# Ring slots of 16 KB a partition, and the experts' weights in rows of 16 KB

## The chip, the cores and the metric

The kernel runs on one core of one Trainium2 chip. A core has five engines that run their own instruction streams: PE (TensorE, matrix products), DVE (VectorE), ACT (ScalarE), POOL (GpSimd) and SP (SyncE, which here does nothing but issue transfers), and 16 DMA engines that move data between HBM and the on-chip memory SBUF, which has 128 partitions. The metric is the device time of one execution in microseconds, the median of three runs. The profiler takes one execution more, and its trace is what is read below.

## The reference

Two transformer blocks on 256 tokens of width 1024, in fp32. The first has a token mixer (differential attention beside a gated linear recurrence, with a context of 256 tokens) and then a mixture of experts in which each expert chooses its tokens:

```
aff = softmax(h @ w_router)                       # 256 tokens x 16 experts
top_aff, top_idx = top_k(aff.T, 32)               # each expert takes 32 tokens
xin = h[top_idx]                                  # 16 x 32 x 1024
y = (silu(xin @ w_gate) * (xin @ w_up)) @ w_down  # each w: 1024 x 1024 per expert
out = scatter_add(y * top_aff)                    # back to the tokens
```

Each expert has three matrices of 4 MB (MB is 2^20 bytes where nothing else is said), so the 16 have 192 MB. The second block has two layers, an attention with a low-rank projection and one with a window, each with a cross attention to a memory of 256 rows and an MLP of width 4096 with squared relu; a last norm follows.

## The kernel before

The work stands in three stages: the mixer of the first block (`first_mixer`, about 0 to 345 us), routing and experts (`route` and `experts`, to about 820 us), and the second block.

All large weights come through one object, the `Ring` (L76). `queue_loads` (L1634) lists every load in the order in which it will be used. `open` fills the slots of a pool as the pool is made; after that `done(key)`, called behind the last matmul that reads a piece, frees its slot and puts the next load of the list into it (`load`, DMA at L99, issued by SP). That load waits on SP for the semaphore of that last matmul. A slot has 2048 floats in each of the 128 partitions, 1 MB. The numbers of slots stand in one line at the file's end: RA 3 slots for the whole run, RE 7 in the mixer only, 4 (`ringB`) from the end of the mixer on, RX 6 from then until after expert 1, RC 5 and RD 3 from the end of the mixer until after expert 13. So when the experts start, the ring has 21 slots, later 15, and in the second block 7.

An expert (loop at L1007 in `experts`) has 32 tokens, so PE's array is used in four column groups of 32: the groups j work on four quarters of the 1024 hidden columns at once. The loop over q takes a quarter of the 1024 rows of gate, then the same quarter of up, 1 MB each; after each comes a `ring.done`. Such a quarter is 8 products, which the trace shows as 16 PE instructions, as each fp32 product is two. The product's moving operand is a piece of a row of weights (`w`), the stationary operand the tokens (`xin`). Then silu and product on ACT and DVE (`ge`, L1031 to L1035), a transpose through PE (`hT`, copied to `hs`), and the down product in four pieces of 1 MB (`pd`, L1049), each with its `done`. `sT`, copied to `S`, is the matrix that scatters the 32 rows back; `eacc` (L1058) adds the expert's rows `yp` into four accumulators that live through all experts.

For expert 0 each quarter gathers its tokens first (`gather`, tile `gp`, L932); the tokens of experts 4 to 9 are gathered behind expert 1 and those of 10 to 15 behind expert 2. From expert 4 on, pieces of the memory's projections (`memory_kv`) stand behind experts as side work. Behind the last expert comes a norm (`rms_add`), and the second block begins with the transposes `ntp` (L1146).

Of the kernel before, what the change touches and what calls it, by code (L numbers as in the profile page):

```python
# [9 lines left out]
F32 = mybir.dt.float32  # L10
# [9 lines left out]
P = 128  # L20
# [55 lines left out]
class Ring:  # L76


    def __init__(self, nc):
        self.nc = nc  # L80
        self.queue = []
        self.held = {}
        self.closed = set()
        self.n = 0

    def want(self, key, src, part=0, parts=1):

        self.queue.append((key, src, part, parts))

    def load(self, pool):  # L90

        self.n += 1
        t = pool.tile([P, 2048], F32, tag="ring", name=f"ring{self.n}")
        while True:
            key, src, part, parts = self.queue.pop(0)
            _, kk, n = src.shape
            if not part:
                self.held[key] = t[:, : parts * kk * n].rearrange("p (k n) -> p k n", k=parts * kk), pool
            self.nc.sync.dma_start(self.held[key][0][:, part * kk:part * kk + kk], src)  # L99
            if not self.queue or not self.queue[0][2]:  # L100
                break

    def open(self, pool, n):
# [8 lines left out]
        return self.held[key][0]  # L112

    def done(self, *key, later=False):
        _, pool = self.held.pop(key)
        if self.queue and id(pool) not in self.closed:
            if later:
                self.later = pool
            else:
                self.load(pool)  # L120


class K:
# [132 lines left out]
def first_mixer(k, perm, st, ringA):  # L256

    nc, tc, A, ring = k.nc, k.tc, k.A, k.ring
# [30 lines left out]
    ident, vecT, x = st["ident"], st["vecT"], st["x"]  # L289
# [11 lines left out]
    for name, r0, nr in (("b_ada", 0, 8), ("norm_pre_mix", 8, 4)):  # L301
        src = A[name]
# [422 lines left out]
        nc.scalar.copy(vd[tk], pts[tk])  # L725

    es_h.close()
    ringB = st["es_b"].enter_context(tc.tile_pool(name="ringB", bufs=4, side="right", reuse_waits="tile"))
    st["ringX"] = st["es_x"].enter_context(tc.tile_pool(name="ringX", bufs=RX, side="right", reuse_waits="tile"))
    ring.open(st["ringX"], RX)  # L730
    ring.open(ringB, 4)


    def first_gate(i):
# [258 lines left out]
def experts(k, st, moe, pool, ps, routed, side):  # L993

    nc, A, ring = k.nc, k.A, k.ring
    ident, x = k.ident, st["x"]
    iot, aff, slot, xin, gather = routed

    def wk(name, shape=(P, 512)):
        return ps.tile(list(shape), F32, tag="mm", bufs=4, name=k.nm(name))  # L1000

    def small(name, shape, dt=F32, bufs=2):
        return pool.tile(list(shape), dt, tag=name, bufs=bufs, name=k.nm(name))


    acc = [[ps.tile([P, 512], F32, tag="acc", bufs=4, name=k.nm("eacc")) for _ in range(2)] for _ in range(2)]
    for e in range(16):  # L1007
        es_ = slice(32 * e, 32 * e + 32)
        pg, pu = wk("pg", (P, 256)), wk("pu", (P, 256))
        for q in range(4):  # L1010
            if e == 0:
                for hk in (2 * q, 2 * q + 1):
                    gather(hk, 0, 4)
            for nm, pt in (("gate", pg), ("up", pu)):
                w = ring.get(nm, e, q // 2, q % 2)
                for kk in range(2):
                    hk = 2 * q + kk
                    for j in range(4):
                        nc.tensor.matmul(pt[32 * j:32 * j + 32, :], lhsT=xin[:, hk, es_], rhs=w[:, kk, 256 * j:256 * j + 256],  # L1019
                                         start=hk == 0, stop=hk == 7)  # L1020
                ring.done(nm, e, q // 2, q % 2)

        sT = wk("sT", (P, 256))
        for T in range(2):
            rep = small("rep", (P, P))
            nc.vector.tensor_scalar(rep.rearrange("p (a b) -> p a b", a=4), iot[:, None, :].to_broadcast([P, 4, 32]), slot[:, T, e:e + 1], aff[:, T, e:e + 1], op0=ALU.is_equal, op1=ALU.mult)
            nc.tensor.transpose(sT[:, T * P:T * P + P], rep, ident)
        S = small("S", (P, 256))
        nc.scalar.copy(S, sT)
        ge = small("ge", (P, 256))  # L1030
        nc.scalar.activation(ge, pg, AF.Exp, scale=-1.0)  # L1031
        nc.scalar.activation(ge, ge, AF.Ln, bias=1.0)
        nc.scalar.activation(ge, ge, AF.Exp, scale=-1.0)  # L1033
        nc.vector.tensor_tensor(ge, ge, pg, op=ALU.mult)  # L1034
        nc.vector.tensor_tensor(ge, ge, pu, op=ALU.mult)  # L1035

        ht = wk("hT", (P, 256))
        for c in range(2):
            nc.tensor.transpose(ht[:, c * P:c * P + P], ge.rearrange("p (n c) -> p c n", c=2)[:, c, :], ident)
        hs = small("hs", (P, 256))  # L1040
        nc.scalar.copy(hs, ht)

        pd = wk("pd")
        for g in range(4):
            wd = ring.get("down", e, g)
            for c in range(2):
                for n in range(2):
                    j = 2 * n + c
                    nc.tensor.matmul(pd[32 * j:32 * j + 32, :], lhsT=hs[:, c * P + 32 * g:c * P + 32 * g + 32],  # L1049
                                     rhs=wd[:, c, n * 512:n * 512 + 512], start=g == 0, stop=g == 3)  # L1050
            ring.done("down", e, g)
        yp = small("yp", (P, 512))
# [581 lines left out]
def queue_loads(k):  # L1634
# [37 lines left out]
    for e in range(16):  # L1672
        gv = A["w_gate"][0, e].rearrange("(h p k) n -> p h k n", h=2, k=4)
        uv = A["w_up"][0, e].rearrange("(h p k) n -> p h k n", h=2, k=4)
        for h in range(2):
            for i in range(2):
                ring.want(("gate", e, h, i), gv[:, h, 2 * i:2 * i + 2])
                ring.want(("up", e, h, i), uv[:, h, 2 * i:2 * i + 2])
        dv = A["w_down"][0, e].rearrange("(g p k) n -> p g k n", g=4, k=2)
        for g in range(4):  # L1680
            ring.want(("down", e, g), dv[:, g])
        if e in (SM + 1, SM + 3):
            cols(("memkv", (e - SM) // 2), A["w_mem_kv_2"][(e - SM) // 2], 0)
    mi = A["mla_w_in_2"][0].rearrange("(h p k) n -> p h k n", h=2, k=4)
# [2 lines left out]
    for i in range(3):  # L1687
        ring.want(("uq", i), A["mla_w_uq_2"][0].rearrange("(k p) n -> p k n", p=P)[:, i:i + 1])
    for i in range(2):
        ring.want(("ukv", i), A["mla_w_ukv_2"][0].rearrange("(k p) n -> p k n", p=P)[:, i:i + 1])  # L1690
    for l in range(2):
        if l:
            for b in (2, 1, 0):
# [116 lines left out]
```

## Time and profile before

| | us |
|---|---|
| median of three runs | 1404.04 (1404.03 to 1404.29) |
| the profiled execution | 1401.51 |
| its span (first to last instruction) | 1399.7 |
| PE busy | 1234.6 (88%) |
| PE weight loads (PEld, beside PE) | 901.0 (64%) |
| DVE busy | 686.8 (49%) |
| ACT busy | 559.8 (40%) |

SP's loads (DMA queue q1) are 346.86 MB (of 10^6 bytes) and took 66.0% of the 16 DMA engines' span. Busy shares are means over three stages with different limits, so they don't tell what a change in one stage is worth; the rows below cut the span into pieces. A matmul row has the tile it writes, an arrow and what it reads; "128x256 f32 x16" is the shape read and the count of instructions.

### The profile page before, as it was taken

The page shows a single profiled execution, that of the slowest core. Times are in us where ns is not written, and L with a number is a line of the kernel's source. Part 1 is how long each engine was busy: PE and PEld are TensorE (multiplying, and loading weights), DVE is VectorE, ACT ScalarE, POOL GpSimd, SP SyncE. Part 2 cuts the span into 40 slices and gives each one's busy share as a digit, 9 for nine tenths or more (in the row PEclk, how much of TensorE's full clock was granted, in tenths as well). Part 3 has the DMA queues.
Part 4 walks back from the last instruction along what each step waited for, and adds up shares of the span by engine and source line. Part 5 has one row for each costly group of instructions (what it writes and reads, how often), then busy time and mean ns, then how long its engine had stood idle before and what let it go on. Part 6 is the DMA issues. An engine that isn't in the chain of part 4 may idle for free.

```text
span 1399.7 us, 21652 instructions
## 1 busy us (share of the span) xinstructions
PE 1234.6 (88%) x8547; PEld 901.0 (64%) x8547; DVE 686.8 (49%) x1549; ACT 559.8 (40%) x1279; POOL 63.3 (5%) x101
## 2 busy tenths in 40 slices
PE   5999997998698668787766779999999999999997
PEld 4876676865454224343222258899899888989995
DVE  5566686667412111110100058666565766665655
ACT  3466233465112112121100147556455645555554
POOL 1111000000000000000000011100000003000000
PEclk9999999999899888898888689999999999999999
DMA  9723864654799999999999963435655542356540
GB/s 311 273 90 124 271 207 128 236 210 176 323 419 420 419 420 420 419 420 420 420 420 420 419 268 105 168 121 181 195 180 197 162 148 91 121 184 204 179 140 31
DMA packets 91969, 352.07 MB, mean 252 GB/s; under 512 B 7041, under 2 KB 15906, under 8 KB 66780
## 3 DMA queue, kind: packets, MB, share of 16 engines
q1 hardware_dynamic: 89760, 346.86, 66.0%
q0 software_dynamic: 1344, 3.21, 0.9%
q8 instruction: 67, 1.10, 0.3%
q10 hardware_dynamic: 764, 0.63, 0.1%
q14 instruction: 34, 0.28, 0.1%
HBM read 349.62 MB, written 1.05 MB: 251 GB/s over the span
## 4 chain that ended last, share of the span: by engine, by line
PE 63%; DMA 27%; DVE 6%; ACT 3%; issue 1%; POOL 0%; ACTq 0%; SPq 0%; DVEq 0%; POOLq 0%
DMA ring<-in_w_up_dram 14%; PE macc L173 13%; PE mpu L173 12%; DMA ring<-in_w_down_dram 10%; PE pj L173 9%; PE oacc L173 3%; PE sp L597 2%; PE spu L173 2%; PE gp L932 2%; PE ob L1190 2%; DMA ring<-in_w_gate_dram 1%; PE pg L1019 1%; PE pa L184 1%; PE acc L173 1%; PE pe L567 1%; PE pu L1019 1%
## 5 line engine op out<-in xcount | busy, mean ns | idle before, releaser
L166 DVE TENSOR_TENSOR wlo<-ring,whi 128x512 fp32r<-128x512 f32 (+3 forms) x459 | 302.4, 665 | 236.6 <-ACT whi L165 235.8
L165 ACT CAST whi<-ring 128x512 fp32r<-128x512 f32 (+3 forms) x465 | 272.7, 594 | 280.2 <-PE macc L173 78.0
L173 PE MATMUL mpu<-h,whi 128*128 128x256 f32 x1024 | 183.6, 280 | 0.0
L173 PE MATMUL macc<-whi,a 128*128 128x512 f32 x512 | 163.1, 395 | 0.0
L173 PEld LDWEIGHTS mpu<-h,whi 128*128 128x128 f32 x1024 | 157.3, 188 | 0.9 <-ACT whi L165 0.3
L173 PE MATMUL mpu<-h,wlo 128*128 128x256 f32 x512 | 142.5, 280 | 0.6 <-DVE wlo L166 0.6
L173 PE MATMUL pj<-whi,hT 128*128 128x512 f32 x416 | 135.7, 400 | 0.5 <-ACT kc L678 0.5
L173 PEld LDWEIGHTS macc<-whi,a 128*128 128x128 f32 x512 | 96.0, 188 | 22.8
L1019 PE MATMUL pu<-ring,xin 128*32 128x256 f32 x1024 | 81.1, 435 | 26.7 <-DMA ring<-in_w_up_dram 26.7
L1019 PE MATMUL pg<-ring,xin 128*32 128x256 f32 x1024 | 81.7, 435 | 24.2 <-DMA ring<-in_w_gate_dram 24.2
L173 PE MATMUL macc<-wlo,a 128*128 128x512 f32 x256 | 101.1, 395 | 0.0
L173 PEld LDWEIGHTS mpu<-h,wlo 128*128 128x128 f32 x512 | 96.1, 188 | 1.6 <-DVE wlo L166 1.0
L1049 PE MATMUL pd<-ring,hs 128*32 128x512 f32 x512 | 77.2, 704 | 18.0 <-DMA ring<-in_w_down_dram 10.5
L173 PEld LDWEIGHTS pj<-whi,hT 128*128 128x128 f32 x416 | 78.3, 190 | 18.3 <-ACT whi L165 1.1
L173 PE MATMUL pj<-wlo,hT 128*128 128x512 f32 x208 | 83.0, 399 | 0.0
L1019 PEld LDWEIGHTS pg<-ring,xin 128*32 128x32 f32 x1024 | 31.1, 120 | 71.2 <-DMA ring<-in_w_gate_dram 38.0
L1019 PEld LDWEIGHTS pu<-ring,xin 128*32 128x32 f32 x1024 | 33.5, 121 | 66.0 <-DMA ring<-in_w_up_dram 44.2
L1034 DVE TENSOR_TENSOR ge<-ge,pg 128x256 f32<-128x256 f32 x16 | 6.7, 420 | 139.0 <-ACT ge L1033 139.0
L1058 PE MATMUL eacc<-yp,S 64*128 64x512 f32 x128 | 48.5, 753 | 20.2 <-DVE yp L1054 20.2
L1031 ACT ACTIVATE ge<-pg 128x256 f32<-128x256 f32 x16 | 6.2, 384 | 130.1 <-PE pg L1019 130.1
L173 PEld LDWEIGHTS macc<-wlo,a 128*128 128x128 f32 x256 | 48.0, 188 | 11.0
L1058 PEld LDWEIGHTS eacc<-yp,S 64*128 64x128 f32 x128 | 21.7, 222 | 45.0 <-DVE yp L1054 34.1
(491 smaller groups left out, 1932.2 us busy)
## 6 DMA issues: line engine op xcount, KB each, us to landing
ring<-in_w_gate_dram SPq DMA_DIRECT2D x64, 1024.0 KB, 9.9
ring<-in_w_up_dram SPq DMA_DIRECT2D x64, 1024.0 KB, 19.9
ring<-in_w_down_dram SPq DMA_DIRECT2D x64, 1024.0 KB, 19.9
ring<-in_mlp_w_up_dram SPq DMA_DIRECT2D x32, 1024.0 KB, 6.0
ring<-in_mlp_w_down_dram SPq DMA_DIRECT2D x32, 1024.0 KB, 5.0
ring<-in_w_ada_dram SPq DMA_DIRECT2D x24, 1024.0 KB, 5.8
ring<-in_w_in_dram SPq DMA_DIRECT2D x32, 512.0 KB, 4.2
ring<-in_w_o_dram SPq DMA_DIRECT2D x8, 1024.0 KB, 5.0
```

What stands on the lines that cost most here:

```text
L165: nc.scalar.copy(view(hi[:, :n]), raw)
L166: (eng or nc.vector).tensor_tensor(view(lo[:, :n]), raw, view(fl(hi[:, :n])), op=ALU.subtract)
L173: self.nc.tensor.matmul(out, lhsT=av if a_st else wv, rhs=wv if a_st else av, start=first and i == 0, stop=last and i == 2)
L184: nc.tensor.matmul(pa[32 * g:32 * g + 32, :], lhsT=k.cs[:, 4 * h + g, :], rhs=w[:, g, :], start=h == 0, stop=h == 1)
L567: nc.tensor.matmul(pe.rearrange("p a b -> p (a b)"), lhsT=part[:, hs], rhs=hgm[:, d, 4 * half:4 * half + 4].rearrange("p a b -> p (a b)"), ...
L597: nc.tensor.matmul(sp[:, T, i - a, :], lhsT=kl, rhs=ql, start=True, stop=True)
L932: nc.tensor.matmul(gp, lhsT=x[:, T, :].rearrange("p (h n k) -> p h k n", h=2, k=4)[:, h, kk, :], rhs=oh[:, T].rearrange("p e s -> p (e s)" ...
L1019: nc.tensor.matmul(pt[32 * j:32 * j + 32, :], lhsT=xin[:, hk, es_], rhs=w[:, kk, 256 * j:256 * j + 256], start=hk == 0, stop=hk == 7)
L1034: nc.vector.tensor_tensor(ge, ge, pg, op=ALU.mult)
L1049: nc.tensor.matmul(pd[32 * j:32 * j + 32, :], lhsT=hs[:, c * P + 32 * g:c * P + 32 * g + 32], rhs=wd[:, c, n * 512:n * 512 + 512], start=g ...
L1058: nc.tensor.matmul(acc[T][n], lhsT=S[ns, T * P:T * P + P], rhs=yp[ns, :], start=e == 0, stop=e == 15)
L1190: nc.tensor.matmul(self.ob[:, T, n, :], lhsT=pt[:, b * P:b * P + P], rhs=val(c), start=i == 0, stop=i == len(blocks[T]) - 1)
```

## The change

A slot is now 4096 floats a partition, 2 MB, in two halves. Each half holds what a slot held; the slot is free when both halves are done. The pools are resized: RA 2, RE 3, RB 2 (the 4 of `ringB`), RC 3, RD 1, RX 3: 22 MB at the start of the experts, 16 MB later, 8 MB in the second block.

The experts' loads are listed in pairs: two neighbouring 1 MB pieces of one matrix are moved by one DMA with rows of 16 KB (`pair`), where before each was a DMA with rows of 8 KB. The order of the list changes with it: gate's first half, up's first half, gate's second, up's second, down's two halves (before, gate and up alternated by 1 MB). The other weights are loaded as before, two loads to a slot.

For w_down a row of 16 KB holds four neighbouring rows of the matrix, so a partition must hold four neighbouring hidden columns. Therefore the column groups j no longer take quarters of the hidden columns but every fourth one: the moving operand of gate and up is now read with a step of 4 floats. The transposes `hT` read a contiguous half where they read every second column. S, ge, hs and yp have one buffer each instead of two.

The core of the diff:

```diff
@@ class Ring
     def load(self, pool):
         self.n += 1
-        t = pool.tile([P, 2048], F32, tag="ring", name=f"ring{self.n}")
-        while True:
-            key, src, part, parts = self.queue.pop(0)
+        t = pool.tile([P, 4096], F32, tag="ring", name=f"ring{self.n}")
+        slot = self.n, pool
+        self.left[slot] = 0
+        halves = [t[:, 0:2048], t[:, 2048:4096]]
+        done = None
+        while self.queue and (halves or self.queue[0][2]):
+            key, src, part, parts, pair, last = self.queue.pop(0)
             _, kk, n = src.shape
             if not part:
-                self.held[key] = t[:, : parts * kk * n].rearrange("p (k n) -> p k n", k=parts * kk), pool
-            self.nc.sync.dma_start(self.held[key][0][:, part * kk:part * kk + kk], src)
-            if not self.queue or not self.queue[0][2]:
+                self.held[key] = halves.pop(0)[:, : parts * kk * n].rearrange("p (k n) -> p k n", k=parts * kk), slot
+                self.left[slot] += 1
+            if pair is not None and len(halves) == 1:
+                self.nc.sync.dma_start(t.rearrange("p (k n) -> p k n", k=2 * kk), pair)
+                done = self.queue[0][0]
+            elif key != done:
+                self.nc.sync.dma_start(self.held[key][0][:, part * kk:part * kk + kk], src)
+            if last:
                 break
...
     def done(self, *key, later=False):
-        _, pool = self.held.pop(key)
-        if self.queue and id(pool) not in self.closed:
+        _, slot = self.held.pop(key)
+        self.left[slot] -= 1
+        if not self.left[slot] and self.queue and id(slot[1]) not in self.closed:
@@ experts
-                        nc.tensor.matmul(pt[32 * j:32 * j + 32, :], lhsT=xin[:, hk, es_], rhs=w[:, kk, 256 * j:256 * j + 256],
+                        nc.tensor.matmul(pt[32 * j:32 * j + 32, :], lhsT=xin[:, hk, es_], rhs=w[:, kk, :].rearrange("p (n j) -> p j n", j=4)[:, j, :],
...
-        for c in range(2):
-            nc.tensor.transpose(ht[:, c * P:c * P + P], ge.rearrange("p (n c) -> p c n", c=2)[:, c, :], ident)
+        for g in range(2):
+            nc.tensor.transpose(ht[:, g * P:g * P + P], ge[:, g * P:g * P + P], ident)
...
-        for g in range(4):
-            wd = ring.get("down", e, g)
-            for c in range(2):
-                for n in range(2):
-                    j = 2 * n + c
-                    nc.tensor.matmul(pd[32 * j:32 * j + 32, :], lhsT=hs[:, c * P + 32 * g:c * P + 32 * g + 32],
-                                     rhs=wd[:, c, n * 512:n * 512 + 512], start=g == 0, stop=g == 3)
-            ring.done("down", e, g)
+        for g in range(2):
+            for i in range(2):
+                wd = ring.get("down", e, g, i)
+                for c in range(2):
+                    o = g * P + 32 * (2 * i + c)
+                    for n in range(2):
+                        j = 2 * n + c
+                        nc.tensor.matmul(pd[32 * j:32 * j + 32, :], lhsT=hs[:, o:o + 32],
+                                         rhs=wd[:, c, n * 512:n * 512 + 512], start=g + i == 0, stop=g + i == 2)
+                ring.done("down", e, g, i)
@@ queue_loads
-            for i in range(2):
-                ring.want(("gate", e, h, i), gv[:, h, 2 * i:2 * i + 2])
-                ring.want(("up", e, h, i), uv[:, h, 2 * i:2 * i + 2])
-        dv = A["w_down"][0, e].rearrange("(g p k) n -> p g k n", g=4, k=2)
-        for g in range(4):
-            ring.want(("down", e, g), dv[:, g])
+        dv = A["w_down"][0, e].rearrange("(h p k) n -> p h k n", h=2, k=4)
+        for name, vs in (("gate", (gv, 0)), ("up", (uv, 0)), ("gate", (gv, 1)), ("up", (uv, 1)), ("down", (dv, 0)), ("down", (dv, 1))):
+            v, h = vs
+            for i in range(2):
+                ring.want((name, e, h, i), v[:, h, 2 * i:2 * i + 2], pair=None if i else v[:, h])
@@
-RA, RE, RC, RD, RX, WB = 3, 7, 5, 3, 6, 4
+RA, RE, RB, RC, RD, RX, WB = 2, 3, 2, 3, 1, 3, 4
```

On SP, before, these are the last loads that go into newly opened slots and the first ones that wait for a slot to come free behind PE (a `ring_` tile is one slot's use, after the arrow the matrix, in brackets the semaphores waited for):

```order
L99 DMA ring_3253<-in_w_up_dram 128x2048 [waits DMAHW0_49]
L99 DMA ring_3255<-in_w_down_dram 128x2048 [waits DMAHW1_49,PE_49]
L99 DMA ring_3387<-in_w_down_dram 128x2048 [waits DMAHW2_49,PE_49]
L99 DMA ring_3397<-in_w_down_dram 128x2048 [waits DMAHW3_49,PE_49]
L99 DMA ring_3415<-in_w_down_dram 128x2048 [waits DMAHW4_49,PE_49]
L99 DMA ring_3425<-in_w_gate_dram 128x2048 [waits DMAHW5_49,PE_49]
```

After, the same place on SP:

```order
L108 DMA ring_3209<-in_w_gate_dram 128x4096 [waits DVE_49,PE_49]
L108 DMA ring_3211<-in_w_up_dram 128x4096 [waits DVE_49,Activation_49]
L108 DMA ring_3213<-in_w_down_dram 128x4096
L108 DMA ring_3369<-in_w_down_dram 128x4096 [waits DMAHW0_49,PE_49]
L108 DMA ring_3379<-in_w_gate_dram 128x4096 [waits DMAHW1_49,PE_49]
```

The first reload before is ring_3387, of 1 MB, behind expert 0's first gate quarter; after it is ring_3369, of 2 MB, behind the second gate quarter, which is the second half of its slot.

On PE, at the end of the last expert, before (`x8` counts products that stand one behind the other, each two instructions in the trace):

```order
L1019 MATMUL pg_5937<-ring_5804,xin_3361 32x256 x8
L1019 MATMUL pu_5938<-ring_5823,xin_3361 32x256 x8
L1019 MATMUL pg_5937<-ring_5833,xin_3361 32x256 x8
L1019 MATMUL pu_5938<-ring_5843,xin_3361 32x256 x8
L1019 MATMUL pg_5937<-ring_5853,xin_3361 32x256 x8
L1019 MATMUL pu_5938<-ring_5863,xin_3361 32x256 x8
L1039 MATMUL hT_6028<-ident,ge_6022 128x128 x2
L1049 MATMUL pd_6033<-ring_5873,hs_6031 32x512 x4
L1049 MATMUL pd_6033<-ring_5883,hs_6031 32x512 x4
L1049 MATMUL pd_6033<-ring_5971,hs_6031 32x512 x4
L1049 MATMUL pd_6033<-ring_5981,hs_6031 32x512 x4
```

And after, the same place on PE:

```order
L1032 MATMUL pg_5723<-ring_5588,xin_3319 32x256 x16
L1032 MATMUL pu_5724<-ring_5598,xin_3319 32x256 x16
L1040 MATMUL sT_5797<-ident,rep_5798 128x128
L1040 MATMUL sT_5797<-ident,rep_5801 128x128
L1032 MATMUL pg_5723<-ring_5633,xin_3319 32x256 x16
L1032 MATMUL pu_5724<-ring_5667,xin_3319 32x256 x16
L1052 MATMUL hT_5812<-ident,ge_5806 128x128 x2
L1064 MATMUL pd_5817<-ring_5714,hs_5815 32x512 x8
L1064 MATMUL pd_5817<-ring_5749,hs_5815 32x512 x8
```

From expert 3 on, gate and up now stand in two groups each instead of four, and down in two instead of four, so eight products instead of four stand behind the last slot. In experts 0 to 2 gate and up still change by quarters.

## Rows read from the trace of the kernel before

**Rows 1.** The page, 40 slices of the span: GB/s moved by DMA.
```profile
GB/s 311 273 90 124 271 207 128 236 210 176 323 419 420 419 420 420 419 420 420 420 420 420 419 268 105 168 121 181 195 180 197 162 148 91 121 184 204 179 140 31
```
**Rows 2.** The page, the chain that ended last, by engine and by line.
```profile
PE 63%; DMA 27%; DVE 6%; ACT 3%; issue 1%; POOL 0%; ACTq 0%; SPq 0%; DVEq 0%; POOLq 0%
DMA ring<-in_w_up_dram 14%; PE macc L173 13%; PE mpu L173 12%; DMA ring<-in_w_down_dram 10%; PE pj L173 9%; PE oacc L173 3%; PE sp L597 2%; PE spu L173 2%; PE gp L932 2%; PE ob L1190 2%; DMA ring<-in_w_gate_dram 1%; PE pg L1019 1%; PE pa L184 1%; PE acc L173 1%; PE pe L567 1%; PE pu L1019 1%
```
**Rows 3.** Windows: us, PE, PEld, DVE, ACT, POOL busy (instructions), clock, DMA share, GB/s.
```profile
400.00:500.00 100.00, 79.28 (x774) 44.07 (x766) 18.54 (x51) 21.28 (x54) 1.12 (x2) 0.92 1.01 419
...
700.00:800.00 100.00, 68.16 (x598) 23.31 (x590) 6.38 (x15) 8.00 (x19) 0.00 (x0) 0.78 1.01 420
```
**Rows 4.** The same view, the second block.
```profile
850.00:1400.00 550.00, 537.96 (x3472) 477.86 (x3470) 358.49 (x737) 300.85 (x683) 28.34 (x48) 1.00 0.46 150
```
**Rows 5.** The same view, where the experts begin.
```profile
362.00:364.00 2.00, 0.90 (x5) 0.82 (x5) 1.73 (x8) 0.00 (x0) 0.00 (x0) 0.50 0.00 0
364.00:366.00 2.00, 2.00 (x15) 1.42 (x14) 1.79 (x8) 0.46 (x1) 0.00 (x0) 0.50 0.00 0
366.00:368.00 2.00, 2.00 (x28) 1.02 (x24) 0.48 (x3) 0.00 (x1) 0.00 (x0) 0.59 0.03 8
...
370.00:372.00 2.00, 2.00 (x31) 1.07 (x34) 0.01 (x1) 0.46 (x1) 0.00 (x0) 1.00 1.02 430
```
**Rows 6.** Timeline of SP from 360 us: start, us, line, load, count.
```profile
367.43 4.64 SPq L99 DMA_DIRECT2D ring<-in_w_down_dram  x3
```
**Rows 7.** Timeline of PE, expert 0: start, us, line, tile, shapes, count.
```profile
365.44 1.94 PE L1019 MATMUL pg<-ring,xin 128*32 128x256 f32 x16
...
370.43 1.26 PE L1019 MATMUL pg<-ring,xin 128*32 128x256 f32 x16
371.50 1.05 PE L1019 MATMUL pu<-ring,xin 128*32 128x256 f32 x16
```
**Rows 8.** Windows as in rows 3, early in the mixer.
```profile
30.00:35.00 5.00, 5.00 (x51) 3.78 (x50) 3.35 (x12) 1.94 (x4) 0.00 (x0) 1.00 1.08 358
```
**Rows 9.** Timeline of PE, the last expert's down product and behind it.
```profile
807.80 1.83 PE L1049 MATMUL pd<-ring,hs 128*32 128x512 f32 x8 [0.50 <-DMA ring<-in_w_down_dram]
...
812.78 1.06 PE L1049 MATMUL pd<-ring,hs 128*32 128x512 f32 x8 [0.92 <-DMA ring<-in_w_down_dram]
814.65 4.04 PE L1058 MATMUL eacc<-yp,S 64*128 64x512 f32 x8 [0.81 <-DVE yp L1054]
```
**Rows 10.** Timeline of PE, expert 2 with the gather behind it.
```profile
413.11 1.07 PE L1019 MATMUL pg<-ring,xin 128*32 128x256 f32 x16
...
418.31 1.05 PE L1019 MATMUL pg<-ring,xin 128*32 128x256 f32 x16
...
430.00 6.39 PE L932 MATMUL gp<-oh,x 128*128 128x192 f32 x26
436.32 1.07 PE L1019 MATMUL pg<-ring,xin 128*32 128x256 f32 x16
```
**Rows 11.** Timeline of PE, a product with a two-step moving operand.
```profile
27.94 1.12 PE L211 MATMUL pa<-ring,cs 128*32 128x128 f32 x32
```
**Rows 12.** Groups of weight loads: line, tile, shape, count | busy us, mean ns | idle before.
```profile
L173 PEld LDWEIGHTS mpu<-h,whi 128*128 128x128 f32 x1024 | 157.3, 188 | 0.9 <-ACT whi L165 0.3
...
L932 PEld LDWEIGHTS gp<-oh,x 128*128 128x128 f32 x96 | 23.0, 328 | 5.6 <-issue 5.6
...
L1146 PEld LDWEIGHTS ntp<-ident,x 128*128 128x128 f32 x64 | 9.5, 213 | 6.4 <-DVE x L253 6.0
...
L1039 PEld LDWEIGHTS hT<-ident,ge 128*128 128x128 f32 x32 | 5.0, 207 | 22.9 <-DVE ge L1035 17.7 <-issue 3.6 <-ACT S L1029 1.6
...
L1027 PEld LDWEIGHTS sT<-ident,rep 128*128 128x128 f32 x32 | 3.2, 140 | 6.6 <-issue 6.6
```

More of the change, by code (lines that the diff above doesn't have):

```diff
@@ L83, in __init__, with want @@
         self.closed = set()
+        self.left = {}
         self.n = 0
-    def want(self, key, src, part=0, parts=1):
-        self.queue.append((key, src, part, parts))
+    def want(self, key, src, part=0, parts=1, pair=None, last=False):
+        self.queue.append((key, src, part, parts, pair, last))
     def load(self, pool):
         self.n += 1
-        t = pool.tile([P, 2048], F32, tag="ring", name=f"ring{self.n}")
-        while True:
-            key, src, part, parts = self.queue.pop(0)
+        t = pool.tile([P, 4096], F32, tag="ring", name=f"ring{self.n}")
[5 more added lines that the diff above has]
+            key, src, part, parts, pair, last = self.queue.pop(0)
             _, kk, n = src.shape
             if not part:
-                self.held[key] = t[:, : parts * kk * n].rearrange("p (k n) -> p k n", k=parts * kk), pool
-            self.nc.sync.dma_start(self.held[key][0][:, part * kk:part * kk + kk], src)
-            if not self.queue or not self.queue[0][2]:
+                self.held[key] = halves.pop(0)[:, : parts * kk * n].rearrange("p (k n) -> p k n", k=parts * kk), slot
[6 more added lines that the diff above has]
+            if last:
                 break
@@ L114, in done @@
     def done(self, *key, later=False):
-        _, pool = self.held.pop(key)
-        if self.queue and id(pool) not in self.closed:
+        _, slot = self.held.pop(key)
+        self.left[slot] -= 1
+        if not self.left[slot] and self.queue and id(slot[1]) not in self.closed:
             if later:
-                self.later = pool
+                self.later = slot[1]
             else:
-                self.load(pool)
+                self.load(slot[1])
 class K:
@@ L727, in first_mixer @@
     es_h.close()
-    ringB = st["es_b"].enter_context(tc.tile_pool(name="ringB", bufs=4, side="right", reuse_waits="tile"))
+    ringB = st["es_b"].enter_context(tc.tile_pool(name="ringB", bufs=RB, side="right", reuse_waits="tile"))
     st["ringX"] = st["es_x"].enter_context(tc.tile_pool(name="ringX", bufs=RX, side="right", reuse_waits="tile"))
     ring.open(st["ringX"], RX)
-    ring.open(ringB, 4)
+    ring.open(ringB, RB)
     def first_gate(i):
@@ L1027, in experts @@
             nc.tensor.transpose(sT[:, T * P:T * P + P], rep, ident)
-        S = small("S", (P, 256))
+        S = small("S", (P, 256), bufs=1)
         nc.scalar.copy(S, sT)
-        ge = small("ge", (P, 256))
+        ge = small("ge", (P, 256), bufs=1)
         nc.scalar.activation(ge, pg, AF.Exp, scale=-1.0)
@@ L1037, in experts @@
         ht = wk("hT", (P, 256))
-        for c in range(2):
-            nc.tensor.transpose(ht[:, c * P:c * P + P], ge.rearrange("p (n c) -> p c n", c=2)[:, c, :], ident)
-        hs = small("hs", (P, 256))
+        for g in range(2):
+            nc.tensor.transpose(ht[:, g * P:g * P + P], ge[:, g * P:g * P + P], ident)
+        hs = small("hs", (P, 256), bufs=1)
         nc.scalar.copy(hs, ht)
         pd = wk("pd")
-        for g in range(4):
-            wd = ring.get("down", e, g)
-            for c in range(2):
-                for n in range(2):
-                    j = 2 * n + c
-                    nc.tensor.matmul(pd[32 * j:32 * j + 32, :], lhsT=hs[:, c * P + 32 * g:c * P + 32 * g + 32],
-                                     rhs=wd[:, c, n * 512:n * 512 + 512], start=g == 0, stop=g == 3)
-            ring.done("down", e, g)
-        yp = small("yp", (P, 512))
+        for g in range(2):
[8 more added lines that the diff above has]
+                ring.done("down", e, g, i)
+        yp = small("yp", (P, 512), bufs=1)
         for n, copy in enumerate((nc.vector.tensor_copy, nc.scalar.copy)):
@@ L1674, in queue_loads @@
         uv = A["w_up"][0, e].rearrange("(h p k) n -> p h k n", h=2, k=4)
-        for h in range(2):
+        dv = A["w_down"][0, e].rearrange("(h p k) n -> p h k n", h=2, k=4)
+        for name, vs in (("gate", (gv, 0)), ("up", (uv, 0)), ("gate", (gv, 1)), ("up", (uv, 1)), ("down", (dv, 0)), ("down", (dv, 1))):
+            v, h = vs
             for i in range(2):
-                ring.want(("gate", e, h, i), gv[:, h, 2 * i:2 * i + 2])
-                ring.want(("up", e, h, i), uv[:, h, 2 * i:2 * i + 2])
-        dv = A["w_down"][0, e].rearrange("(g p k) n -> p g k n", g=4, k=2)
-        for g in range(4):
-            ring.want(("down", e, g), dv[:, g])
+                ring.want((name, e, h, i), v[:, h, 2 * i:2 * i + 2], pair=None if i else v[:, h])
         if e in (SM + 1, SM + 3):
@@ L1689, in queue_loads @@
     for i in range(2):
-        ring.want(("ukv", i), A["mla_w_ukv_2"][0].rearrange("(k p) n -> p k n", p=P)[:, i:i + 1])
+        ring.want(("ukv", i), A["mla_w_ukv_2"][0].rearrange("(k p) n -> p k n", p=P)[:, i:i + 1], last=i == 1)
     for l in range(2):
```

## The prediction

> **What bounds the kernel now.** I read first the page's slices and its chain of waits. In the slices the reader is to see three stretches: about 345 us in which the transfers come and go, a plateau of 419 to 420 GB/s, and a last part in which they are mostly idle [rows 1]. The chain gives 27% of the span to DMA, nearly all of it the experts' up and down weights, and 63% to PE, whose lines are those of the mixer and of the second block [rows 2]. The windows settle which of the two holds each stage: from 400 to 500 us the DMA engines are full (share 1.01, 419 GB/s) while PE is busy 79 of 100 us, from 700 to 800 us 68 of 100 [rows 3]; from 850 to 1400 us it is the other way round, PE 538 of 550 us with the DMA share at 0.46 [rows 4]. So a change of the ring is worth something in the middle stage alone: by its rate, by the hole in the stream where the stage begins, and by what follows its last transfer. "MB" below is 2^20 bytes, 2.50 us at 420 GB/s.
>
> The hole is seen in narrow windows: nothing moves from 362 to 366 us, 8 GB/s until 368, the full rate by 370 to 372 [rows 5]. The ring is full, and SP's first load after it is issued at 367.43 [rows 6], when PE is through with the gate quarter that it began at 365.44 [rows 7].
>
> **The rate of the stream.** Of the experts' 192 MB, 170 follow the hole, 170 x 2.50 = 425 us. Rows of 8 KB become rows of 16 KB; no row shows one. The nearest are the short ones: from 30 to 35 us the engines are full (1.08) at 358 GB/s [rows 8] with w_ada's rows of 1 KB and w_in's of 2 KB, two MB of the former to each half MB of the latter, 1138 B on the mean. At 16 engines that is 51 ns a row, and 312 ns for 8 KB at 420 GB/s. The straight line through the two is 9.1 ns and 0.0370 ns a byte, so 16 KB would take 615 ns instead of 624: 1.45%, or 6.1 us of the 425. The other end is nothing, if the engines' limit is in the bytes by then, or if a row of 16 KB is moved in pieces. I take -5 us, near the line's end, since the step from 1 to 8 KB did pay by that line. [...]
>
> **The head.** The ring now opens 11 slots of 2 MB, 22 MB in place of 21, so the stream runs 2.5 us longer before it is full. The first slot comes free not with the first gate quarter but with the second, which shares the slot: today that group begins at 370.43 and the next, up, at 371.50 [rows 7]; with about 0.2 us to the issue, 371.7 in place of 367.43, +4.3 us. Two MB are asked for then and two more a microsecond later, so the stream is full at once, as it is now. Head: +4.3 - 2.5 = +1.8 us. If the slots before it are opened later than now, the 2.5 us are lost; if the later half of the gate isn't what is waited for, the 4.3 are not paid: between 0 and +4.3.
>
> **The tail.** The last load is 2 MB, and 16 PE instructions stand behind its landing instead of 8. Eight took 1.06 us at 812.78 and 1.83 us at 807.80, the clock between the two levels (0.78 of the 2.4 GHz from 700 to 800 us) [rows 3, 9]. So it costs +0.9 (by the spacing of the groups below, 0.86) to +1.8 us; I take +1.3. What comes behind (yp, the four eacc products, the norm) is the same chain. The waits inside an expert don't count: an expert's groups are as many as before, and PE has 20 to 30 us of idle time in 100.
>
> **The strided operand.** Gate and up now read every fourth float of a row of weights as the moving operand, 8 groups of 16 PE instructions in each expert. Contiguous, a group of 16 (256 columns) takes 0.86 us to the next: from 413.11 to 418.31 six steps [rows 10]. Step 2 is in the trace: L211 runs 32 instructions of 128 columns, as much work, in 1.12 us against 1.05 for the contiguous group [rows 10, 11], so step 2 is free. Step 4 shows only in weight loads: gp's, which read x with it, take 328 ns against 188 for mpu's contiguous ones, 1.74 times; of the transposes ntp with step 4 takes 213 against 140 for the contiguous sT, and hT with step 2 takes 207 [rows 12]. Weight loads therefore pay for any step, and for 4 nearly what they pay for 2; as moving operands pay nothing for 2, I take nothing for 4. The other end is 1.74 times, worked out in the first rival, and up to 2.3 times, if a moving read with step costs what the two-step transpose shows per column ((207-140) ns over 128 on top of the 0.42 ns of a column). Nothing hides the groups in experts 0 to 2, where PE sets the pace; behind them PE's idle time does. [...]
>
> **The rest.** hT's weight loads become contiguous (207 to 140 ns, two an expert, where PE waits for a transfer anyway). S, ge, hs and yp fall from two buffers to one; each is written after the previous expert's products on PE, which is in order, and beside a DMA wait: nothing. SP issues half as many loads for the experts. In the mixer the ring holds ten MB as before, freed two at a time; of the chain's 27% DMA the lines of rows 2 leave 2% for all else, so nothing; if two MB were wanted before they are there, it is up to 5 us. In the second block the ring has 8 MB in place of 7 and PE shows no wait for it [rows 4]: nothing; if slots of 2 MB came free too late there, a load of 2 MB is 5 us, but the DMA share of 0.46 leaves twice that.
>
> Sum: -5 + 1.8 + 1.3 = -1.9 us. The profiled execution took 1401.51 us (span 1399.7 and 1.8 around it), so 1399.6 by its clock; the median of the runs is 2.5 us above it, 1404.04, and the same -1.9 gives 1402.1. Of this case alone, with rate 0 to -6.1, head 0 to 4.3 and tail 0.9 to 1.8: about 1399 to 1405, the corners left out.
>
> **Rivals.** *The strided operand is slow, s times* (slower than before). Gate and up of an expert take 8 x 0.86 = 6.9 us, so each grows by 6.9(s-1). Experts 0 to 2 are paced by PE; expert 3 starts at 436.32 [rows 10] and would start 20.7(s-1) later. By then the ring is full again: 36 MB are used up to there and 16 MB are held, 52 together, and with 22 MB there when it starts again, at about 373 us, the other 30 MB are there at 373 + 75 = 448. Up to s = 1 + 11.7/20.7 = 1.57 nothing is lost; from there the stream stands still for 20.7(s-1) - 11.7: 3.6 us at 1.74, 9.0 at 2, 15 at 2.3. Above about 2 an expert that has side work like the gather (an expert takes 436.32-413.11 = 23.2 us of PE with it) is longer than its 12 MB, 30.0 us, and adds some more. On top of -1.9: 1405.7 at 1.74, about 1411 at 2, 1417 to 1421 at 2.3. For it: the weight loads; against it: step 2. Chance 0.28 up to 2.2 (at 1411), 0.08 above (at 1420).
>
> *Rows of 16 KB bring no rate* (the change doesn't do what it says): head and tail remain, +3.1 us, 1407.1. For it: share 1.01 at 420 GB/s all along, whatever PE does; against it: the line of rows 8. Chance 0.10.
>
> *More is gained*: the line's whole 6.1 us, and a head that costs nothing because the slots open earlier or PE, with fewer and longer groups, lets the stream run on: 1396 to 1400, say 1398. For it: 430 GB/s shows in the window from 370 to 372 us [rows 5]. Chance 0.12.
>
> **How the numbers follow.** The forecast's case has 0.42, and its time, 1402.1, is the prediction. 0.2% is 2.8 us, about what a measurement of this kernel can tell from no change: faster is below 1401.2, slower above 1406.8. The first case divides as 0.16 faster, 0.25 same, 0.01 slower, the slow operand as 0 : 0.05 : 0.31 (its lower s come out the same), no rate as 0 : 0.01 : 0.09, more gained as 0.12 : 0 : 0. Sum 0.28 faster, 0.31 same, 0.41 slower. The range leaves out the slowest operand and the greatest gain: 1397 to 1417.
>
> **What would show it.** Rate: the plateau from 400 to 800 us at 424 to 426 GB/s with a share near 1.0; at 420 this step is wrong. Head: the hole from about 364.5 to 372, and SP's first load behind it near 371.7. Tail: sixteen pd instructions behind the last landing. Operand: groups of 16 in expert 2 still 0.86 us apart; if 1.5 us or more, or if the DMA rate dips before 450 us, the first rival holds. Wrong altogether if the second block's 540 us of PE change by more than a microsecond.

## The result, and the profile after

The changed kernel takes 1416.97 us (median of 4 runs, 1416.51 to 1418.35) against 1404.03 for the one before: ratio 1.0095, 95% interval 1.0078 to 1.0113. It is slower by 13 us, where 2 us faster was forecast. The profiled execution took 1416.51 us with a span of 1414.4, 14.7 longer than before.

The windows of the kernel after (columns as in rows 3) show first the hole at the start of the experts, then the plateau and four dips in it (384 to 400, 440 to 460, 460 to 480 and 520 to 540 us):

```profile
364.00:366.00 2.00, 0.36 (x2) 0.28 (x2) 1.38 (x6) 0.00 (x0) 0.00 (x0) 0.50 0.94 401
366.00:368.00 2.00, 1.68 (x7) 1.71 (x8) 1.79 (x8) 0.00 (x0) 0.00 (x0) 0.50 0.06 25
368.00:370.00 2.00, 2.00 (x19) 0.92 (x21) 1.50 (x7) 0.46 (x1) 0.00 (x0) 0.50 0.00 0
...
374.00:376.00 2.00, 2.00 (x18) 0.74 (x21) 0.00 (x0) 0.46 (x1) 0.00 (x0) 1.00 0.00 0
376.00:378.00 2.00, 2.00 (x20) 0.45 (x12) 0.00 (x0) 0.00 (x0) 0.00 (x0) 1.00 0.62 115
...
384.00:400.00 16.00, 14.29 (x102) 5.58 (x106) 2.36 (x6) 3.00 (x7) 0.00 (x0) 1.00 0.93 378
...
440.00:460.00 20.00, 18.03 (x115) 10.55 (x107) 3.91 (x9) 4.08 (x9) 0.00 (x0) 1.00 0.88 357
460.00:480.00 20.00, 18.90 (x162) 5.98 (x165) 1.48 (x5) 3.42 (x7) 0.00 (x0) 1.00 0.84 342
520.00:540.00 20.00, 19.00 (x142) 5.80 (x144) 2.69 (x8) 1.96 (x5) 0.00 (x0) 0.89 0.78 313
...
600.00:700.00 100.00, 95.92 (x756) 42.20 (x759) 16.03 (x39) 18.41 (x46) 1.00 (x2) 1.00 1.01 426
700.00:800.00 100.00, 88.06 (x622) 26.93 (x618) 8.76 (x20) 10.40 (x25) 0.00 (x0) 0.94 1.01 427
```

Where the stream runs it moves 426 to 427 GB/s, against 420 [rows 3]. But the hole lasts about 11 us, where it was between 6 and 8 [rows 5], and from 440 to 480 and from 520 to 540 us the DMA engines stand still for an eighth to over a fifth of the time (shares 0.88, 0.84 and 0.78), while PE is busy 18 to 19 of 20 us. Against 427 GB/s these three windows lose 3.3, 4.0 and 5.3 us, and the one from 384 to 400 us loses 1.8.

What PE does there stands in its timeline, which answers to rows 7, 9 and 10 (expert 0, expert 2 and the end; in brackets the idle time before a group and what ended it):

```profile
368.46 2.02 PE L1032 MATMUL pg<-ring,xin 128*32 128x256 f32 x16
370.28 2.01 PE L1032 MATMUL pu<-ring,xin 128*32 128x256 f32 x16
...
374.28 2.00 PE L1032 MATMUL pg<-ring,xin 128*32 128x256 f32 x16
...
429.41 1.99 PE L1032 MATMUL pg<-ring,xin 128*32 128x256 f32 x16
431.20 2.02 PE L1032 MATMUL pu<-ring,xin 128*32 128x256 f32 x16
...
442.14 2.04 PE L1032 MATMUL pu<-ring,xin 128*32 128x256 f32 x16
...
827.12 2.81 PE L1064 MATMUL pd<-ring,hs 128*32 128x512 f32 x16 [2.65 <-DMA ring<-in_w_down_dram]
830.72 4.45 PE L1073 MATMUL eacc<-yp,S 64*128 64x512 f32 x8 [0.79 <-DVE yp L1069]
838.13 3.81 PE L1161 MATMUL ntp<-ident,x 128*128 128x128 f32 x16 [2.97 <-DVE x L266]
```

In expert 2 eight groups begin 1.82 us apart ((442.14 - 429.41) / 7), 2.1 times the 0.87 of rows 10. The first group of expert 0 shows the same 1.82 at the granted clock 0.50 of its window. There the contiguous one took 1.70, from 365.44 [rows 7] to this row of the kernel before:

```profile
367.14 1.29 PE L1019 MATMUL pu<-ring,xin 128*32 128x256 f32 x16
```

So the step costs 0.12 us a group where the granted clock is 0.50 (0.50 and 0.59 in the two windows of the contiguous one [rows 5]). In expert 2, where it is 1.00 in every window of 2 us from 428 to 444 us, the step costs 0.95, 1.82 against 0.87, and so takes away what the faster clock gives. SP's timeline of the kernel after gives the first reload:

```profile
376.34 0.33 SPq L108 DMA_DIRECT2D ring<-in_w_down_dram  x1
```

That is 7.9 us behind the first gate group (368.46), against 2.0 before (rows 6 and 7). One more wait grew, between 225 and 255 us in the mixer. DVE waits there for the small vectors of lambda (us in total, times, longest), first in the kernel before, then in the one after:

```profile
DVE lp L648 <- DMA lv<-in_da_lambda_k_dram: 7.7, 2, 6.4
DVE lp L661 <- DMA lv<-in_da_lambda_k_dram: 10.0, 2, 6.6
```

PE stands idle behind it, 6.55 us before and 8.84 after, until it can begin the rotary transposes `tp`:

```profile
243.99 1.09 PE L515 MATMUL tp<-ident,ro 128*128 128x128 f32 x4 [6.55 <-DVE ro L672]
247.62 1.09 PE L528 MATMUL tp<-ident,ro 128*128 128x128 f32 x4 [8.84 <-DVE ro L685]
```

### The profile page after: what moved, and what is told of

Same layout as the page of the kernel before. It is cut to its first block, busy times and chain, and to the rows that moved or that the text cites. A ratio compares the mean times of both kernels' runs of the same rounds, so it can differ in the third digit from the quotient of the medians.

```text
span 1414.4 us, 21418 instructions
## 1 busy us (share of the span) xinstructions
PE 1307.7 (92%) x8547; PEld 904.9 (64%) x8547; DVE 685.9 (48%) x1549; ACT 559.8 (40%) x1279; POOL 61.9 (4%) x101
## 4 chain that ended last, share of the span: by engine, by line
PE 56%; DMA 4%; DVE 2%; ACT 1%; issue 1%; ACTq 0%; DVEq 0%
PE macc L186 12%; PE mpu L186 12%; PE pg L1032 5%; PE pu L1032 5%; DMA ring<-in_w_down_dram 4%; PE oacc L186 3%; PE pd L1064 3%; PE eacc L1073 2%; PE pk L186 2%; PE spu L186 2%; PE ob L1205 2%; PE ptp L1248 1%; PE ssc L1636 1%; PE uq L186 1%; PE csc L1284 1%; PE msc L1545 1%
## 5 line engine op out<-in xcount | busy, mean ns | idle before, releaser
L1032 PE MATMUL pu<-ring,xin 128*32 128x256 f32 x1024 | 127.7, 633 | 3.0 <-DMA ring<-in_w_up_dram 3.0
L1032 PE MATMUL pg<-ring,xin 128*32 128x256 f32 x1024 | 127.3, 631 | 0.8 <-DMA ring<-in_w_gate_dram 0.8
L1032 PEld LDWEIGHTS pu<-ring,xin 128*32 128x32 f32 x1024 | 39.4, 128 | 81.4 <-issue 75.6
L1032 PEld LDWEIGHTS pg<-ring,xin 128*32 128x32 f32 x1024 | 34.9, 124 | 71.6 <-issue 67.2
L1039 DVE TENSOR_SCALAR rep<-iot,slot,aff 128x128 f32<-128x128 f32 x32 | 9.9, 344 | 145.4 <-PE sT L1040 145.4
L1064 PE MATMUL pd<-ring,hs 128*32 128x512 f32 x512 | 66.0, 646 | 13.0 <-ACT hs L1054 7.4
L1042 ACT COPY S<-sT 128x256 f32<-128x256 f32 x16 | 6.0, 372 | 121.3 <-PE sT L1040 121.3
L186 PE MATMUL oacc<-whi,oT 128*128 128x512 f32 x128 | 46.2, 412 | 0.0
```

What stands on the lines that cost most here:

```text
L186: self.nc.tensor.matmul(out, lhsT=av if a_st else wv, rhs=wv if a_st else av, start=first and i == 0, stop=last and i == 2)
L1064: nc.tensor.matmul(pd[32 * j:32 * j + 32, :], lhsT=hs[:, o:o + 32], rhs=wd[:, c, n * 512:n * 512 + 512], start=g + i == 0, stop=g + i == 2)
```

## The experiments

In each the time is the median of the timed runs, and the kernel before, run beside them, took 1402.8 to 1403.0.

**The moving operand, pairs of neighbours.** Two hidden columns of each four go to a group, so that both floats lie in the same 16 bytes; the transposes read every second column again.

```diff
-rhs=w[:, kk, :].rearrange("p (n j) -> p j n", j=4)[:, j, :],
+rhs=w[:, kk, 512 * (j // 2):512 * (j // 2) + 512].rearrange("p (n i c) -> p i n c", i=2, c=2)[:, j % 2],
...
-o = g * P + 32 * (2 * i + c)
+o = c * P + 32 * (2 * g + i)
```

> The kernel after, but the four column groups take the hidden columns so that the moving operand reads two neighbouring floats of every four (columns 512h + 4p + 2i + c, with h and i from the group and c running innermost) instead of one float of every four; rows of 16 KB, slots, order and down product stay. Theory A (a moving read that finds only one float in each 16 bytes is what doubled a group from 0.86 to 1.82 us): groups of 16 in expert 2 are 0.86 us apart again, the stream stays at 426 to 428 GB/s from 400 us on, and the time falls by the stall of 11 us and what experts 4 to 9 lost, to 1401 to 1405. Rival B (any moving pattern with a step of 16 bytes in it is slow, neighbours or not): groups stay near 1.8 us, 1417. Rival C (the groups are slow because rows of 16 KB land in SBUF beside them, whatever the step): 1.8 us, 1417. Left of the slowdown in any case: +3.0 us in the mixer and the later first reload.

1401.73 us, 15.2 less than the change, ratio to before 0.9991 (0.9983 to 1.0000). In expert 2, and from 440 to 460 us:

```profile
419.60 1.11 PE L1032 MATMUL pg<-ring,xin 128*32 128x256 f32 x16
420.52 1.09 PE L1032 MATMUL pu<-ring,xin 128*32 128x256 f32 x16
```
```profile
440.00:460.00 20.00, 16.64 (x182) 9.46 (x183) 4.44 (x12) 5.40 (x13) 0.00 (x0) 0.98 1.01 428
```

The groups are 0.91 us apart (0.92 in this pair) and the dip is gone, with rows, slots and order as in the change. The rivals B and C of the expectation fall. This kernel is called the pair kernel below.

**The step alone, in the kernel before.**

```diff
-rhs=w[:, kk, 256 * j:256 * j + 256],
+rhs=w[:, kk, :].rearrange("p (n j) -> p j n", j=4)[:, j, :],
```

> The kernel before (rows of 8 KB, 1 MB slots) with one edit: gate and up read every fourth float as the moving operand. The hidden columns reach w_down in another order, so this part of the output is not the reference's; instruction counts and shapes are the same. Theory A: groups of 16 take 1.82 us in expert 2 and the kernel gets slower: expert 3 would start 8 x 3 x 0.96 = 23 us later, the ring's 15 MB are full from about 445 us, so 15 us lost there and some more in experts 4 to 9: 1418 to 1425. Rival C (rows of 16 KB are the cause): groups 0.86, 1404. A mixer that is 3 us faster than the changed kernel's in any case.

1418.83 us, ratio 1.0115 (1.0099 to 1.0130): +16 us without any row of 16 KB. Its expert 2:

```profile
426.79 2.00 PE L1019 MATMUL pg<-ring,xin 128*32 128x256 f32 x16
428.58 2.05 PE L1019 MATMUL pu<-ring,xin 128*32 128x256 f32 x16
```

**Other patterns**, one per quarter in experts 0 and 2 of the pair kernel.

```diff
+kind = {0: ("step1", "step4", "pair1", "step1"), 2: ("step3", "step2", "pair3", "step8")}.get(e, ("pair0",) * 4)[q]
```

> The kernel with two neighbouring floats of four, in which expert 0 and expert 2 read their moving operands in other patterns, a quarter each (the same number of columns; the columns read are not the right ones, so their part of the output is not the reference's). Expert 0: step 1, step 4, two neighbours of four beginning at the second float, step 1. Expert 2: step 3, step 2, two neighbours of four beginning at the fourth float (each pair lies over the end of 16 bytes), step 8. Theory A (hits in a row on the same 16 bytes count): step 1, step 2 and both pairs 0.86 us from group to group, step 4 and step 8 1.82, step 3 (four floats from three such lines) in between, about 1.5. Rival B (the size of the step counts): step 3 about 1.4, step 8 above 1.82 (up to 3.6), pairs 1.8 since they hold a step of four.

One profile, and no timing that counts. Expert 2: the first two groups step 3, then two of step 2, two of pairs over a 16-byte end (the first shown), two of step 8:

```profile
419.62 1.56 PE L1049 MATMUL pg<-ring,xin 128*32 128x256 f32 x16
420.99 1.59 PE L1049 MATMUL pu<-ring,xin 128*32 128x256 f32 x16
422.38 1.12 PE L1049 MATMUL pg<-ring,xin 128*32 128x256 f32 x16
423.29 1.11 PE L1049 MATMUL pu<-ring,xin 128*32 128x256 f32 x16
424.19 1.13 PE L1049 MATMUL pg<-ring,xin 128*32 128x256 f32 x16
...
426.05 2.04 PE L1049 MATMUL pg<-ring,xin 128*32 128x256 f32 x16
427.88 2.06 PE L1049 MATMUL pu<-ring,xin 128*32 128x256 f32 x16
```

From group to group step 2 takes 0.91 us, the pairs 0.92, step 3 1.37 and step 8 1.83, no more than step 4. (In expert 0, in groups behind a gather, step 4 takes 1.79, pairs from the second float on 1.10 and contiguous columns 1.08.) The 256 columns of an instruction lie in 128 pieces of 16 bytes at step 2, in 192 at step 3 and in 256 at steps 4 and 8, and 0.91, 1.37 and 1.82 stand to each other as 128, 192 and 256. So for the moving operand of these products what counts is how many floats are taken from each 16 bytes, not how far the step goes. One float from each 16 bytes takes 2.1 times the contiguous group (1.82 us against 0.87, both at the granted clock 1.00). A pair that lies over the end of 16 bytes is no slower (0.92 us): its second float and the next pair's first lie in the same 16 bytes.

**Rows of 8 KB**, as DMAs of 1 MB, and as DMAs of 2 MB from two stretches 1 MB apart.

```diff
-pair=None if i else v[:, h])
+pair=None)                                  # 1 MB
+pair=None if i else v8[:, 2 * h:2 * h + 2]) # 2 MB, v8 = w viewed "(g p k) n -> p g k n", g=4
```

> The kernel with two neighbouring floats of four (two_hits, 1401.73 us, stream at 426 to 427 GB/s), but each half slot is loaded by a DMA of its own: 1 MB in rows of 8 KB, the two halves of a slot still one slot. Theory R (the row's length sets the rate, a fixed 9 ns a row): 420 GB/s from 400 us on, so 425 us of stream become 7 us longer: 1408 to 1410. Rival S (the DMA's size, 2 MB instead of 1, sets it): also 420. Rival T (it is the slot, or the fewer waits of SP): 426 to 427, 1401 to 1403.

> As two_hits with one DMA of 2 MB for a slot, but from two stretches 1 MB apart in each matrix, so in rows of 8 KB. The rows of the matrices then stand in another order in the slot than the products take them, so the experts' part of the output is not the reference's; all counts and shapes stay. Theory R (row length): 420 GB/s, 1408 to 1410. Rival S (DMA size): 426 to 427 GB/s, 1401 to 1403.

1406.28 and 1405.22 us (ratios to before 1.0022 and 1.0015), 4.6 and 3.5 more than the pair kernel. The same window, of the 2 MB DMAs in rows of 8 KB:

```profile
500.00:600.00 100.00, 71.06 (x646) 35.79 (x634) 17.62 (x45) 19.86 (x53) 0.00 (x0) 0.88 1.01 420
```

and of the pair kernel, 2 MB in rows of 16 KB:

```profile
500.00:600.00 100.00, 73.03 (x680) 36.98 (x669) 17.31 (x46) 20.04 (x53) 0.00 (x0) 0.86 1.01 426
```

The 1 MB DMAs move 420 GB/s in this window too. So in this stream the row's length sets the rate (420 with 8 KB, 426 with 16 KB); the size of the DMA, the slot and the number of loads do not. The times rose by less than the 7 us expected, but the experts' stage did not: from the first gate group to the last wait for a landing it takes 449.2 and 449.1 us in the two, 442.9 in the pair kernel, 6.3 and 6.2 more. Both kernels win back part of the mixer's loss: PE's wait before the rotary transposes is 6.51 and 6.95 us in them, 8.25 in the pair kernel. With rows of 8 KB ahead of them DVE waits 7.7 and 8.2 us for the small vectors, and 9.5 in the pair kernel. The first also has the shorter tail of loads of 1 MB (1.88 us from the last wait to eacc, 4.04 in the pair kernel). What else the mixer gained in these profiles is open.

**The first slot.** Expert 0's gate and up as 1 MB loads in turn.

```diff
+if e == 0:
+    for n in range(8):
+        name, (v, h) = order[n // 4 * 2 + n % 2]
+        i = n // 2 % 2
+        ring.want((name, e, h, i), v[:, h, 2 * i:2 * i + 2])
+    order = order[4:]
...
```

> two_hits, with expert 0's gate and up listed as in the kernel before: 1 MB loads in rows of 8 KB, gate and up in turn, so that the first slot holds the first quarter of both and comes free behind the first up group, not behind the second gate group. Theory (the hole in the stream from 368 to 379.5 us, 11 us against 7 before, is the slot's second half being used late, and the stream is what ends the stage): the first reload comes 3.4 us earlier after the first expert group, the hole shrinks by as much, 1398 to 1399. Rival (the stream has slack, or SP's next loads follow no earlier): 1401 to 1402.

1396.38 us, ratio 0.9953 (0.9937 to 0.9968), 5.4 less than the pair kernel and 2 more than expected. Its first group begins at 366.86 and its first reload is

```profile
369.99 0.33 SPq L108 DMA_DIRECT2D ring<-in_w_down_dram  x1
```

3.1 us behind it, where the pair kernel needs 6.7 (371.01 to 377.73): 3.6 us, about what was expected. Not all of it reaches the end of the stage. From the first gate group to the last wait for a landing it takes 440.5 us against 442.9, 2.4 less: the stream restarts below its rate (385, 393, 336 and 377 GB/s in the windows of 2 us from 372 to 380). The rest of the 5.4 lies outside this stretch, which I had not foreseen. 1.65 us of it can be named: expert 0's loads are in flight when the lambda vectors are fetched (SP issues three of them from 231.70 to 233.24 us, POOL the vectors from 233.55 on), and as they are now in rows of 8 KB, PE's wait there is 6.60 again instead of 8.25.

**The lambda vectors**, in the kernel before, fetched at the start.

```diff
-lv = ta("lv")[:, 0:256].rearrange("p (a b) -> p a b", a=4)
-for n, name in enumerate(("da_lambda_q1", "da_lambda_k1", "da_lambda_q2", "da_lambda_k2")):
-    nc.gpsimd.dma_start(lv[:, n, :], bcast(A[name], 64))
+lv = st["wrA"].rearrange("p (a x) b -> p a (x b)", a=4)   # filled behind the first loads of the ring
```

> The kernel before with the four vectors for lambda loaded at the start of the kernel instead of behind the mixer's scan, where DVE waits 7.7 us for them (10.0 us in the changed kernel) and PE stands still for 6.5 (8.8). Theory (the changed kernel's +2.1 us at 240 us is these small loads waiting behind two 2 MB loads): PE's idle time before the rotary transposes goes, 4 to 6.5 us faster, 1398 to 1400; beside the same edit on the changed kernel the two mixers then differ by 0.9 us, not 3.0. Rival (something else ends that wait, the POOL queue or the rotary work itself): under 2 us.

1397.48 us, ratio 0.9963 (0.9949 to 0.9977): the wait is real, and without it the kernel before gains 5.3 us on balance. The edit delays the start of this profile by 2.8 us, and still its rotary transposes begin at 240.29 instead of 243.99. The rival falls.

**Where the step costs**: pairs in one part of the experts, the step of four in the other.

```diff
-rhs=w[:, kk, 512 * (j // 2):512 * (j // 2) + 512].rearrange("p (n i c) -> p i n c", i=2, c=2)[:, j % 2],
+rhs=w[:, kk, :].rearrange("p (n j) -> p j n", j=4)[:, j, :] if e < 3 else ...   # and with e >= 3
```

> two_hits (1401.73 us) with the step of four floats in experts 0 to 2 only, pairs of neighbours in experts 3 to 15 (in experts 0 to 2 the hidden columns then reach w_down in another order, so their output is not the reference's). Theory (the first rival's price: PE sets the pace in experts 0 to 2, the ring hides 11.7 us of their 8 x 3 x 0.91 = 22 us, the stream stands still for the rest): +10, 1411 to 1413. Rival (these three fall inside the ring's reserve, and the loss comes later, where side work makes an expert longer than its 12 MB): +0 to 3, 1402 to 1405.

> two_hits with the step of four floats in experts 3 to 15 only (their output is then not the reference's). Theory: behind expert 2 the reserve of the ring is whole, an expert of 7.3 us more is longer than its transfers only where memory side work stands behind it (experts 4 to 9), so the loss is small or nothing on its own: +0 to 5, 1402 to 1407. Rival (the loss of 15 us in the changed kernel is mostly here): +10 or more, 1412.

1409.78 us (+8.1 over the pair kernel, where 10 were expected; ratio to before 1.0052, 1.0037 to 1.0067) and 1401.15 (-0.6). The window of the second one:

```profile
440.00:460.00 20.00, 18.90 (x150) 7.99 (x153) 2.40 (x6) 2.98 (x7) 0.00 (x0) 1.00 1.01 427
```

Thirteen slow experts cost nothing as long as the ring's reserve is whole; three cost 8 us; all sixteen 15.2, not 7.5. What the first three use up the later ones lack: the dips at 460 to 480 and 520 to 540 us appear at this size only when both are slow. From 460 to 480 us the stream moves 401 GB/s with the first three slow, 426 with the rest slow and 342 with all; from 520 to 540 us it is 428, 426 and 313.

**All together.** Pairs, the first slot, the last 2 MB as two DMAs, and the lambda vectors fetched early. The edit shown is that of the last 2 MB.

```diff
-pair=None if i else v[:, h])
+pair=None if i or (name, e, h) == ("down", 15, 1) else v[:, h])
```

> two_hits with the listing of two_hits_e0, the last expert's last 2 MB as two DMAs of 1 MB (the first eight instructions need not wait for the second MB), and the lambda vectors loaded at about 45 us instead of behind the scan (as in before_lv, but past the kernel's first loads, which cost 2.8 us there at the start). If the three costs are separate: 1401.7 - 3.4 - 1 - 7 = 1390 to 1392. If the mixer's gain only moves the hole (the stream is full before the experts begin and restarts with PE): the same, since the restart is PE's; if the stream were limited by the start of its loads, the 7 us would be lost and it ends at 1397.

1390.09 us (1388.88 to 1391.79), ratio 0.9907 (0.9891 to 0.9924): faster than both kernels, 27 us below the change, and within what was expected. One premise did not hold: POOL issues the fetches of the lambda vectors at 5 to 10 us of the trace, not at about 45. The first of them:

```profile
5.23 0.58 POOL L458 DMA_DIRECT2D wrA<-in_da_lambda_q_dram  x1
```

The projections `pj` that begin at 26.88 us in the pair kernel begin at 29.82 here, so the delay at the start is paid here too. Against the kernel with the new first slot (1396.38) the vectors and the tail give 6.3 us, where the vectors alone gave 5.3 in the kernel before and the tail's lines give 1.7. That fits costs that are separate, but it tests their sum and not each of them. Its end:

```profile
803.18 1.07 PE L1064 MATMUL pd<-ring,hs 128*32 128x512 f32 x8 [0.44 <-DMA ring<-in_w_down_dram]
805.05 2.59 PE L1073 MATMUL eacc<-yp,S 64*128 64x512 f32 x8 [0.80 <-DVE yp L1069]
```

1.87 us from the last wait to eacc, as before (812.78 to 814.65, rows 9); the change has 3.60.

## Why the prediction was wrong

The step that failed is the strided operand: "as moving operands pay nothing for 2, I take nothing for 4". They pay 2.1 times for 4, 1.82 us a group where 0.87 was taken. I read the weight loads of rows 12, slow at step 2 and 4 alike, as a sign that moving operands would also treat the two alike. The weight loads here do not go with the moving operand. The trace after has the transposes of `hT` with contiguous columns (ns: least, median, greatest):

```profile
L1052 PEld LDWEIGHTS hT<-ident,ge x32: 137/141/144, 391.3 to 821.7; 128*128 128x128 f32 x32
```

The same 32 loads took 207 ns at step 2 [rows 12], so a weight load pays for step 2, while a moving operand goes from 0.87 to 0.91 us a group. For the moving operand step 2 takes two floats from each 16 bytes (0.91 us a group), step 4 one (1.82), and that is the difference. The first rival, held at 0.28 with about 1411 us, was the case.

The rival's price, 20.7(s-1) - 11.7, gives 11.1 us at 2.1, which makes 1413.2. Experts 0 to 2 alone cost 8.1, less than that, and together with the rest 15.2: its clause on experts above s = 2 "adds some more" was the half that I did not work out.

The rate was right in mechanism and too small: -5 taken, 6.1 the upper bound, while 426 to 427 against 420 GB/s over 425 us is 6 to 7 us. The line through two points was good: its 615 ns for 16 KB are 426 GB/s. (Unrounded it has 8.7 ns a row, not 9.1, and a gain of 5.9 us.) What fell short was the -5 taken below it.

The head was right in mechanism. The first reload came 5.9 us later behind the first group instead of 4.3; without the step in expert 0 it is 4.1 to 4.7 (6.1 to 6.7 us behind the group in four kernels, 2.0 before), so 1.2 to 1.8 are the step's. The tail was +1.7, inside its bounds of 0.9 to 1.8 (1.3 taken). The clock in its estimate is known as a share alone, 0.78 from 700 to 800 us [rows 3]; the 2.4 GHz beside it is no reading of these traces.

The mixer was put at nothing, with a wrong reason: "the ring holds ten MB as before". The pool of the first slots is closed as soon as it is filled, so the ring there lives on the slots of pool A alone, 3 of 1 MB before, 2 of 2 MB now. No run shows that this cost time: between 26 and 226 us PE waits for none of the ring's transfers, in either trace. The first gate group begins 3.0 us later (368.46 against 365.44), and PE's wait behind the lambda vectors is 2.3 us longer. With rows of 16 KB in flight there it is 8.84 us in the change, 8.25 in the pair kernel and 8.36 in the one with other patterns; in the five kernels with 8 KB it is 6.51 to 6.95, the kernel before (6.55) among them. With the vectors fetched at the start the first gate group begins at 361.68 in the kernel before and at 363.07 in the last kernel, 1.4 apart instead of 3.0. The rest is not settled: the profiles of the changed kernels spread over several us at this place, from 365.7 to 371.0 for the first gate group.

Sum for the trace: mixer +3.0, from the first gate group to the last wait for a landing +11.3 (458.7 us against 447.3), tail +1.7, from eacc to the end -1.4; but for rounding this is the 14.7 measured. Of the 11.3 the rate is -7.0, the hole 5.9 - 2.5 = +3.4 and the four dips +14.4, together +10.8. Why the stretch behind eacc is shorter is open. Without the step the parts nearly cancel: the pair kernel stands at 0.9991 of the time before.

## What to carry to other kernels

When a layout hands every n-th element to a matmul, count how many of them lie in the same 16 bytes: here two cost next to nothing (0.91 us a group against 0.87) and one 2.1 times (1.82, at the granted clock 1.00), and with the columns dealt to the groups in pairs the kernel took 0.9991 of the time before. An engine off the critical path can still lose time that the path pays, once its reserve of loaded data is used up (three slow experts cost 8.1 us, thirteen nothing, all sixteen 15.2): price the slowdown where that engine sets the pace, then carry the lost reserve on. Longer rows paid in the full stream (426 GB/s against 420) and cost where a small transfer waits beside it (PE idle 8.25 to 8.84 us against 6.51 to 6.95).

## What the runs showed of the hardware

- Rows of 16 KB, in DMAs of 2 MB, moved 426 to 427 GB/s in the full stream; rows of 8 KB moved 420 from 500 to 600 us, in DMAs of 1 and of 2 MB alike.
- A small transfer beside rows of 16 KB was waited for longer than beside rows of 8 KB: PE idled 8.3 to 8.8 us (three profiles) instead of 6.5 to 7.0 (five) behind four vectors of 256 bytes a partition.
- Moving operand in fp32, 16 instructions of 256 columns in four column groups: 0.87 us contiguous, 0.91 in pairs and 1.82 with step 4, at the granted clock 1.00; at 0.50 step 4 also took 1.82 (contiguous 1.70). In the kernel with other patterns step 2 took 0.91, step 3 1.37 and step 8 1.83. From step 2 on the time went as the number of 16-byte pieces touched (128, 192 and 256 an instruction).
- Weight loads of 128 columns in fp32, the same transposes: 141 ns contiguous, 207 with step 2.
- While PE was busy 96 of 100 us the granted clock was 1.00 (600 to 700 us, after); in the kernel before, busy 79, it was 0.85.
